# Three edits to when loads are issued in a hybrid attention and RWKV-7 block

## The chip, the cores and the metric

The kernel runs on one core of a Trainium2 chip. The metric is device time in microseconds (us) of one execution. PE is TensorE, PEld its weight load, DVE is VectorE, ACT is ScalarE, POOL is GpSimd, SP is SyncE, whose queue issues most DMA transfers. SPq in a row is SP's instruction queue.

## The reference

One decoder block over x (512 tokens, width 1024), all in float32:

```python
proj = rms_norm(x, norm_mix_g) @ w_in
o_nsa = nsa_attention(...)          # 8 heads: compressed, selected and window branch
o_rwkv = rwkv7_time_mix(...)        # 8 heads: recurrence over time, then
                                    # (layer norm of y + bonus) * gate
x = x + concatenate([o_nsa, o_rwkv]) @ w_out
x = x + memory_cross_attention(rms_norm(x, norm_x_g), rms_norm(mem, norm_mem_g), w_q_x, w_kv_x, w_o_x)
h = rms_norm(x, norm_ffn_g)
x = x + (silu(h @ w_gate) * (h @ w_up)) @ w_down
return rms_norm(x, norm_f_g)
```

The bonus is `sum(r * k * r_k) * v` for each head. x enters twice: at the start, and as the residual that is added to the output projection.

## The kernel before

Every large product is made of three: a float32 operand is split into a rounded high half and the remaining low half (`split`, lines L339 and L340: a cast on ACT, a subtraction on DVE), and high by high, high by low and low by high are summed.

The work is written as strands, Python generators that a planner (`Threads`) steps through. `start` loads x and norms it. `bulk` does all weight products, item by item, in the order of the text `ORDER`: r, K, q, v are parts of the input projection, m the compression, X and V the keys and values of the memory, `o00` to `o07` and `o10` to `o17` the output projection (first digit: the half of the tokens; second: the step over its 8 blocks of rows, which take the blocks 0 1 2 4 5 6 7 3), `x` the load of the residual, N the next norm, W a wait. Four strands `pair 0` to `pair 3` prepare the RWKV heads, `inverse` inverts their triangular matrices, `chain` runs the recurrence over 8 chunks and then, in a tail of four rounds, norms it, adds the bonus, multiplies by the gate and makes the output blocks 4 to 7. `attention` makes blocks 0 to 3. `mem` norms the memory.

The planner has a clock of its own, a priority for each strand, counts of free buffers by pool (Q, T, U and others) and a table of pauses (`ADJ`) by strand and number of the step. A strand that yields a dict of counts waits for that many free buffers; one that yields a number pauses. The order in which the planner steps the strands becomes the program order, which is the priority of the instructions. The language's scheduler then simulates the program and fixes the order of each engine's instructions and the buffer that each tile gets. An edge made by `after` orders only the issue: the scheduler places an instruction no earlier than the one named; on the chip nothing waits for it.

`pin` chains each strand's products in their own order; it stores the last product of any strand in `last[0]` and that of the strand in `mine`. `now` orders a load behind `last[0]`. It is used for weight loads (`wload`, L373), the bonus store (L650), the stores of the pairs (L669), the inverse's load (L713), the gate matrix (`gup`, L844) and the bonus loads (`bon`, L848).

The raw weights have two buffers (`tW`), their halves two each. `bulk` makes the halves of item n+1 and issues the load of item n+2 before the products of item n, so a weight load waits for the low half (L340) of the tile two items ahead of it. `xr_load` (L1314) loads the four tiles of x in one item between V03 and o00; they are added to the finished sums in `wout_item` (L1307). In the tail of `chain` each round takes three U buffers, loads the bonus first (L848), makes the variance, its rsqrt (L858, L859), the scaled row (L861, L862), adds the bonus on POOL (L863) and multiplies by the gate (L868). `inverse` stores its result at L729 and L730 and loads it back at L738 and L742.

Of the kernel before, what the change touches and what calls it, by code (L numbers as in the profile page):

```python
# [14 lines left out]
T = 512  # L15
# [43 lines left out]
INV_LAG = 9.0  # L59
DENS = 4500  # L60
PR = {'pair': 50}
ORDER = """L B P0 r00 r01 C1 r02 P1 r10 P2 r11 C0 r12 r21 m0 r20 m1 r22 P3 m2 r31 m3 r30 m4 r32 m5 K0 m6 q0 K1 m7 v0 v1 v2 q1 q3 q2 M X0 X1 X2 X3 X4 X5 X6 X7 V00 V01 V02 V03 x o00 o01 o02 o03 o04 o05 o06 o07 N o10 o11 o12 o13 o14 o15 o16 o17 W V10 V11 V12 V13"""


class Threads:
# [62 lines left out]
def _body(ctx, tc, I, out, dbg=None, upto=99, mark=lambda s: None):  # L128
    nc = tc.nc
# [13 lines left out]
    def mk(tag, bufs, pool=None):  # L143
        def f(shape=(128, 512), dt=F32, n=tag):
            return (pool or pp).tile(list(shape), dt, tag=tag, bufs=bufs, name=nm(n))
        return f
# [7 lines left out]
    tQ = mk("Q", NQ)  # L154
    tT = mk("T", NT)
    tU = mk("U", NU)
# [9 lines left out]
    th = Threads(mark, lambda n: tc.high_priority(n) if n else nullcontext(), Q=NQ - 7, T=NT, U=NU, K=KU, S=2, A=2)  # L166
# [4 lines left out]
    def after(ins, first):  # L171
        tc.add_manual_dep(ins.ins, first.ins.name,
                          mybir.DependencyInfo(mybir.DependencyClass.NoSync, mybir.DependencyReason.DATA), reason="order")
        return ins

    last, mine = [None], {}
# [8 lines left out]

    def now(ins):

        return after(ins, last[0]) if last[0] is not None else ins

    def free(ap):  # L190
        n = 1
# [4 lines left out]
    def mm(o, l, r, start, stop):  # L196
        m, n = free(l), free(r)
        if l.dtype == F32R:
            c = (0.055 if m <= 64 else 0.107) if n <= 128 else n * 0.000422
        elif m <= 32:  # L200
            c = 0.04
        elif m <= 64:
            c = max(0.08, n * 0.0009 + 0.02)
        else:
            c = max(0.214, n * 0.00168)
        th.cols.append((th.clock, n * l.shape[0] / 128 * (1 if l.dtype == F32R else F4)))
        return pin(PE.matmul(o, lhsT=l, rhs=r, start=start, stop=stop, skip_group_check=True), c)  # L207
# [157 lines left out]
    def qpair(n):  # L365
        t = tQ([128, 2, 512], F32R, n=n)
        return t[:, 0, :], t[:, 1, :]
# [203 lines left out]
    bdr = dp.tile([4, 128, 512], F32, name="bdr")  # L571
# [207 lines left out]
    def chain():  # L779
        yield "vt"  # L780

        def own(q):

            for c in (2 * q, 2 * q + 1):
                for j, e, o in HEADS:
                    r = slice(64 - o, 128 - o)
                    mm(pE[o:o + 64, c % 2, j, :], AM[j][e][r, c, 0:64], VT[c // 4][r, c % 4, j, :], True, True)
            z = tU([128, 2, 4, 64], n="zv")
            A.copy(z, pE)
            return z  # L790

        yield "vg"
        yield dict(A=1)
        pE = pA([128, 2, 4, 64], n="zy")
        zv = own(0)
        yield CH_LAG
        p = pC([128, 2, 4, 64], n="ch")
        S = None
        for c in range(8):

            uv = tU([128, 2, 4, 64], n="uv")
            G.tensor_copy(uv[64:128, 0], VT[c // 4][64:128, c % 4])
            G.tensor_copy(uv[0:64, 1], VT[c // 4][0:64, c % 4])
            if c > 0:
                for j, e, o in HEADS:
                    mm(p[o:o + 64, 0, j, :], AR[j][o:o + 64, c, 0:64], S[o:o + 64, j, :], True, True)
                Z = t1([128, 4, 64], n="Z")
                V.tensor_add(Z, p[:, 0], zv[:, c % 2])
            else:
                Z = zv[:, 0]  # L810
            if c % 2 == 1 and c < 7:
                zv = own(c // 2 + 1)
            if c > 0:
                yield CH_LAG
            for j, e, o in HEADS:
                mm(p[o:o + 64, 1, j, :], AM[j][e][o:o + 64, c, 0:64], Z[o:o + 64, j, :], True, True)
            V.tensor_copy(uv[0:64, 0], p[0:64, 1])
            A.copy(uv[64:128, 1], p[64:128, 1])
            if c > 0:
                for j, e, o in HEADS:  # L820
                    mm(pE[o:o + 64, c % 2, j, :], S[o:o + 64, j, :], AR[j][o:o + 64, c, 64:128], j == 0, False)
            yield CH_LAG

            Sn = None
            if c < 7:
                for j, e, o in HEADS:
                    mm(p[o:o + 64, 0, j, :], BKt[j][:, c, e, :], uv[:, e, j, :], True, True)
                Sn = t1([128, 4, 64], n="S")
                if c == 0:
                    V.tensor_copy(Sn, p[:, 0])  # L830
                else:
                    G.tensor_tensor(Sn, S, WC[:, :, c:c + 1].broadcast_to([128, 4, 64]), op=ALU.mult)
                    V.tensor_add(Sn, p[:, 0], Sn)
            for j, e, o in HEADS:
                mm(pE[o:o + 64, c % 2, j, :], uv[:, e, j, :], AM[j][e][:, c, 64:128], c == 0, True)
            A.copy(VT[c // 4][:, c % 4], pE[:, c % 2])
            S = Sn
            yield CH_LAG
        th.done("chain", 1.0)
        th.free(Q=16, U=4, A=1)  # L840

        yield dict(Q=1)
        gup = tQ([128, 512], n="gup")
        now(nc.sync.dma_start(gup, I["rwkv_g_up"][0]))  # L844
        for j in range(4):
            yield dict(U=3, T=2)
            bon, sq, rs = tU(n="bon"), tU(n="ysq"), tU(n="rs")
            now(nc.sync.dma_start(bon, bdr[j]))  # L848
            h2 = [slice(0, 256), slice(256, 512)]
            c4 = lambda x: x.rearrange("p (c t) -> p c t", c=4)  # L850
            for h in range(2):
                A.activation(c4(sq[:, h2[h]]), VT[h][:, :, j, :], AF.Square)
            bs = bsum(sq, "var", tT)
            yield next(bs) + 1.0
            yield dict(s=1)
            p = next(bs)
            th.free(T=2)
            A.activation(rs, p, AF.Ln, bias=kst[:, 1:2], scale=1.0 / 64)  # L858
            A.activation(rs, rs, AF.Exp, scale=-0.5)  # L859
            for h in range(2):  # L860
                V.tensor_mul(c4(rs[:, h2[h]]), c4(rs[:, h2[h]]), VT[h][:, :, j, :])  # L861
            V.tensor_scalar(rs, rs, col("rwkv_lnx_w", j), col("rwkv_lnx_b", j), op0=ALU.mult, op1=ALU.add)  # L862
            G.tensor_tensor(rs, rs, bon, op=ALU.add)  # L863
            yield 6.0
            yield dict(s=1)
            p = pS(n="g")
            mm(p, gup[:, j * 128:(j + 1) * 128], sgd, True, True)
            V.tensor_mul(rs, p, rs)  # L868
            yield dict(Q=1)
            oT[4 + j] = qpair("oT")  # L870
            split(*oT[4 + j], rs)
            th.free(U=3)
            th.done(f"o{4 + j}", 4.0)
        th.free(Q=3)
# [395 lines left out]
    xr, acc = [], {}  # L1270
# [40 lines left out]
                    th.free(Q=8, S=2)  # L1311
        return ld, run

    def xr_load(dep):  # L1314
        for i in range(4):
            xr.append(tQ([128, 1024], n="xr"))
            after(nc.sync.dma_start(xr[i], I["x"][0, i * 128:(i + 1) * 128, :]), dep)

    def norm_all(name, f, g, ev, done):
        name.append(f)  # L1320
# [26 lines left out]
    def xq_part(k):  # L1347
        return [(ALLP, 0, wcols("w_q_x", k * 128, 128))]
# [200 lines left out]
    def call(f, need=None):  # L1549

        def run(W):
            if need:
                yield need
            f()
        return None, run
# [9 lines left out]
    def build(n):  # L1565
        k, i = n[0], [int(c) for c in n[1:]]
        return {"L": lambda: duo(xn1, "xn", ([(ALLP, 0, wcols("w_in", RW0 + 1536, 128))], pA, lora_fin),
                                 ([(ALLP, 0, wcols("w_in", RW0 + 1664, 128))], pA, gd_fin)),
                "P": lambda: spawn_pair(*i), "r": lambda: rkv_item(*i), "B": lambda: call(lambda: th.add(1, "bias", bias(), th.clock)),
                "C": lambda: cv_item(*i), "m": lambda: cmp_item(*i), "K": lambda: k_item(*i),  # L1570
                "v": lambda: vg_item(*((0, 3), (3, 6), (6, 8))[i[0]]), "q": lambda: q_item(*i),
                "M": lambda: call(lambda: th.add(4, "mem", mem_load(last[0]), th.clock)),
                "X": lambda: kx_item(*i), "W": lambda: wait("chain"), "V": lambda: vx_item(*i),
                "x": lambda: call(lambda: xr_load(last[0]), dict(Q=4)),
                "o": lambda: wout_item(*i), "N": lambda: call(x_norm, dict(Q=9))}[k]()

    def x_norm():
# [4 lines left out]

    items = [build(n) for n in ORDER.split()]
    items += [duo(lambda: xn2[0], "xn2", (xq_part(0), pA, xq_fin(0), dict(Q=1)), (xq_part(1), pA, xq_fin(1), dict(Q=1)))] + \
# [55 lines left out]
```

## Time and profile before

| what | us |
|---|---|
| median of 3 runs | 959.26 |
| lowest and highest | 958.56 and 960.78 |
| the profiled execution | 957.83 |
| its span, from the first to the last instruction | 955.5 |

The profiled execution is one run; what lies around its span is 2.33 us. Durations below are from it, and the predicted time is set against the median of the runs.

### The profile page before, as it was taken

Reading aid. Unit: us, or ns where it says so; the run is one execution under the profiler, and the core shown is the slowest. Engines: PE = TensorE matmul, PEld = TensorE weight load, DVE = VectorE, ACT = ScalarE, POOL = GpSimd, SP = SyncE. Lnnn points to the kernel's source line nnn. Section 1 sums busy time; section 2 is a strip of 40 time slices with the busy share of each in tenths; the row PEclk is TensorE's granted clock in tenths of the full one; section 3 lists DMA queues with packets and bytes.
Section 4 is the critical chain, followed back from the end, with each engine's and each line's share of the span. In section 5 each row is a group of like instructions: output and inputs, shape, how many; then the busy total and the mean of one; then the engine's idle time right before and its main releaser. Section 6 shows DMA issues by size and latency. Waiting matters only on the chain.

```text
span 955.5 us, 14534 instructions
## 1 busy us (share of the span) xinstructions
PE 910.5 (95%) x5797; PEld 741.0 (78%) x5797; DVE 508.4 (53%) x991; ACT 401.2 (42%) x738; POOL 81.7 (9%) x128
## 2 busy tenths in 40 slices
PE   6999999999999988799899999999999999999997
PEld 4778777777778766666788888888888888888885
DVE  5366676788566776356655555444343343422235
ACT  4455444347567886234444433332333323212121
POOL 5121110000240010001200002000000000000002
PEclk9999999999999999999999999999999999999999
DMA  7222445636203111754431141333333333242332
GB/s 229 60 63 70 128 108 144 174 89 133 91 2 101 35 56 45 220 176 153 134 88 46 65 139 39 110 89 91 109 88 110 89 90 109 88 131 89 95 105 88
DMA packets 125405, 97.19 MB, mean 102 GB/s; under 512 B 23531, under 2 KB 109873, under 8 KB 125339
## 3 DMA queue, kind: packets, MB, share of 16 engines
q1 hardware_dynamic: 122714, 91.80, 33.2%
q10 hardware_dynamic: 2624, 4.48, 1.7%
q8 instruction: 45, 0.74, 0.3%
q14 instruction: 22, 0.17, 0.1%
HBM read 90.22 MB, written 4.48 MB: 99 GB/s over the span
## 4 chain that ended last, share of the span: by engine, by line
PE 76%; DVE 7%; ACT 6%; DMA 5%; issue 3%; POOL 2%; SPq 0%; POOLq 0%; ACTq 0%; DVEq 0%
PE pj L207 41%; PE acc L207 14%; DMA w<-in_w_out_dram 3%; PE pv L207 2%; DVE wl L340 2%; ACT wh L339 2%; PE sc L207 2%; PE pt L211 2%; PE ps L207 1%; PE vg L207 1%; PE ch L207 1%; DMA w<-in_w_kv_x_dram 1%; PE kx L207 1%; PE xs L207 1%; PE xo L207 1%
## 5 line engine op out<-in xcount | busy, mean ns | idle before, releaser
L207 PE MATMUL pj<-xn,wh 128*128 128x512 f32 (+1 forms) x1280 | 294.3, 378 | 0.5 <-DVE xn L340 0.5
L340 DVE TENSOR_TENSOR wl<-w,wh 128x1024 fp32r<-128x1024 f32 (+1 forms) x130 | 158.4, 1219 | 203.7 <-ACT wh L339 118.9
L207 PEld LDWEIGHTS pj<-xn,wh 128*128 128x128 f32 x1280 | 227.9, 190 | 46.0 <-issue 2.9
L339 ACT CAST wh<-w 128x1024 fp32r<-128x1024 f32 (+1 forms) x131 | 136.9, 1045 | 284.7 <-PE pj L207 144.6
L207 PE MATMUL pj<-xn,wl 128*128 128x512 f32 (+1 forms) x640 | 155.3, 379 | 0.0
L207 PEld LDWEIGHTS pj<-xn,wl 128*128 128x128 f32 x640 | 114.2, 189 | 22.0 <-issue 1.6
L207 PE MATMUL acc<-wh,hid 128*128 128x512 f32 x288 | 68.2, 389 | 0.0
L207 PEld LDWEIGHTS acc<-wh,hid 128*128 128x128 f32 x288 | 54.1, 188 | 11.2
L1475 DVE SCALAR_TENSOR_TENSOR th<-th,pj 128x512 f32<-128x512 f32 x22 | 15.1, 688 | 75.7 <-PE pj L207 75.7
L207 PE MATMUL acc<-wh,oT 128*128 128x512 f32 x128 | 34.6, 410 | 7.1 <-ACT wh L339 4.5
L1105 ACT ACTIVATE S<-S,mx 128x128 f32<-128x128 f32 (+3 forms) x64 | 35.3, 553 | 4.3 <-DVE mx L1103 4.2
L207 PEld LDWEIGHTS acc<-wh,oT 128*128 128x128 f32 x128 | 23.5, 192 | 15.8 <-ACT wh L339 7.9
L207 PE MATMUL acc<-wl,hid 128*128 128x512 f32 x144 | 35.6, 389 | 0.0
L1536 POOL TENSOR_TENSOR xr<-xr,gain 128x512 f32<-128x512 f32 x4 | 5.2, 1290 | 345.4 <-DVE ss L1533 345.4
L1103 DVE CUSTOM_DVE_ANT_0 S<-ps,Bt 128x128 f32<-128x128 f32 (+3 forms) x64 | 29.7, 484 | 8.5 <-PE ps L207 8.3
L207 PE MATMUL ps<-K,q 128*128 128x512 f32 (+2 forms) x96 | 30.1, 395 | 3.4 <-DVE mx L1103 2.3
L207 PEld LDWEIGHTS acc<-wl,hid 128*128 128x128 f32 x144 | 27.0, 188 | 5.6
L207 PE MATMUL pv<-S,Vt 128*64 128x128 f32 x320 | 30.6, 284 | 0.3 <-ACT S L1146 0.2
L211 PE MATMUL pt<-ident,S 128*128 128x128 f32 x160 | 25.8, 280 | 4.2 <-ACT S L1146 4.2
L339 ACT CAST hid<-th 128x512 fp32r<-128x512 f32 x22 | 13.7, 621 | 31.7 <-DVE th L1475 31.7
L280 POOL TENSOR_TENSOR ss<-ss,kst 128x1 f32<-128x1 f32 x14 | 7.7, 552 | 208.3 <-DVE ss L279 208.3
L211 PEld LDWEIGHTS pt<-ident,S 128*128 128x128 f32 x160 | 18.1, 140 | 9.4 <-ACT S L1146 5.3
(298 smaller groups left out, 1303.2 us busy)
## 6 DMA issues: line engine op xcount, KB each, us to landing
w<-in_w_gate_dram SPq DMA_DIRECT2D x22, 512.0 KB, 3.9
w<-in_w_up_dram SPq DMA_DIRECT2D x22, 512.0 KB
w<-in_w_down_dram SPq DMA_DIRECT2D x22, 512.0 KB, 3.4
w<-in_w_in_dram SPq DMA_DIRECT2D x18, 512.0 KB, 5.4
w<-in_w_kv_x_dram SPq DMA_DIRECT2D x16, 512.0 KB, 4.6
w<-in_w_out_dram SPq DMA_DIRECT2D x16, 256.0 KB, 3.9
w<-in_w_out_dram SPq DMA_DIRECT2D x8, 512.0 KB, 5.0
w<-in_w_q_x_dram SPq DMA_DIRECT2D x8, 512.0 KB, 3.9
```

Source lines behind the costliest of these rows:

```text
L207: return pin(PE.matmul(o, lhsT=l, rhs=r, start=start, stop=stop, skip_group_check=True), c)
L211: return pin(PE.transpose(o, i, idn), 0.109 if i.shape[0] > 64 else 0.056)
L280: G.tensor_tensor(ss[:, 1:2], ss[:, 0:1], mhalf, op=ALU.pow)
L339: seq(A, A.copy(H, src))
L340: i = (eng or V).tensor_sub(L, src, v32(H))
L1103: V.tensor_tensor_reduce(out=s, in0=p[:, br - b0], in1=Bt[:, a, n - 1::-1], scale=-1.0, scalar=3e38, op0=ALU.add, op1=ALU.min, accum_out=m ...
L1105: A.activation(s, s, AF.Exp, bias=mx[:, a, br + 1:br + 2], scale=-1.0, accum_out=sm[:, a, br + 1:br + 2])
L1475: V.scalar_tensor_tensor(t, t, 0.5, p, op0=ALU.mult, op1=ALU.mult)
L1536: G.tensor_tensor(x, x, gf[0][:, cs], op=ALU.mult)
```

## The change

A load that went through `now` is ordered behind the last product of its own strand, and behind the last of any strand only if its own has none yet. The bonus is loaded after the row is scaled, and its U buffer is asked for there. The load of the residual becomes four items, one ahead of each pair of the first half's parts of the output projection, each asking for one Q buffer instead of four at once.

```diff
-... V02 V03 x o00 o01 o02 o03 o04 o05 o06 o07 N ...
+... V02 V03 x0 o00 o01 x1 o02 o03 x2 o04 o05 x3 o06 o07 N ...
...
     def now(ins):
 
-        return after(ins, last[0]) if last[0] is not None else ins
+        own = mine.get(th.cur, last[0])
+        return after(ins, own) if own is not None else ins
...
         for j in range(4):
-            yield dict(U=3, T=2)
-            bon, sq, rs = tU(n="bon"), tU(n="ysq"), tU(n="rs")
-            now(nc.sync.dma_start(bon, bdr[j]))
+            yield dict(U=2, T=2)
+            sq, rs = tU(n="ysq"), tU(n="rs")
...
             V.tensor_scalar(rs, rs, col("rwkv_lnx_w", j), col("rwkv_lnx_b", j), op0=ALU.mult, op1=ALU.add)
+            yield dict(U=1)
+            bon = tU(n="bon")
+            now(nc.sync.dma_start(bon, bdr[j]))
             G.tensor_tensor(rs, rs, bon, op=ALU.add)
...
-    def xr_load(dep):
-        for i in range(4):
-            xr.append(tQ([128, 1024], n="xr"))
-            after(nc.sync.dma_start(xr[i], I["x"][0, i * 128:(i + 1) * 128, :]), dep)
+    def xr_load(i, dep):
+        xr.append(tQ([128, 1024], n="xr"))
+        after(nc.sync.dma_start(xr[i], I["x"][0, i * 128:(i + 1) * 128, :]), dep)
...
-                "x": lambda: call(lambda: xr_load(last[0]), dict(Q=4)),
+                "x": lambda: call(lambda: xr_load(*i, last[0]), dict(Q=1)),
```

## Rows read from the trace of the kernel before

**Rows 1.** The page's first part: busy us (share of the span) xinstructions.
```profile
PE 910.5 (95%) x5797; PEld 741.0 (78%) x5797; DVE 508.4 (53%) x991; ACT 401.2 (42%) x738; POOL 81.7 (9%) x128
```
**Rows 2.** Windows: stretch, length, busy us by engine, granted clock, DMA share, GB/s.
```profile
240.00:300.00 60.00, 59.01 (x1086) 47.70 (x1085) 38.02 (x128) 37.05 (x105) 16.21 (x31) 1.00 0.19 62
...
395.00:410.00 15.00, 12.13 (x44) 9.36 (x45) 4.70 (x5) 3.10 (x3) 0.00 (x0) 0.89 0.73 240
...
600.00:825.00 225.00, 225.00 (x995) 186.27 (x993) 89.19 (x105) 69.03 (x84) 0.00 (x0) 1.00 0.34 98
```
**Rows 3.** Waits of PE, 20 to 380: us in total, times, longest.
```profile
PE ps L207 <- DVE mx L1103: 2.3, 1, 2.3
...
PE kx L207 <- ACT wh L339: 0.6, 1, 0.6
```
**Rows 4.** Waits of PE, 380 to 470.
```profile
PE acc L207 <- ACT wh L339: 4.5, 6, 2.3
PE acc L207 <- DVE vx L340: 2.7, 1, 2.7
PE acc L207 <- DVE wl L340: 1.6, 2, 1.1
```
**Rows 5.** Timeline of PE, 386 to 426: start, us, work [idle before <-releaser].
```profile
402.01 1.07 PE L207 MATMUL acc<-wl,oT 128*128 128x512 f32 x4
405.38 2.11 PE L207 MATMUL acc<-wh,oT 128*128 128x512 f32 x8 [2.30 <-ACT wh L339]
...
408.23 1.98 PE L207 MATMUL acc<-wh,oT 128*128 128x512 f32 x8
...
411.47 2.11 PE L207 MATMUL acc<-wh,oT 128*128 128x512 f32 x8 [0.36 <-ACT wh L339]
...
417.72 2.12 PE L207 MATMUL acc<-wh,oT 128*128 128x512 f32 x8 [0.51 <-ACT wh L339]
```
**Rows 6.** Timeline of ACT, 402 to 424.
```profile
404.28 2.05 ACT L339 CAST wh<-w 128x1024 fp32r<-128x1024 f32 x2 [7.02 <-DMA w<-in_w_out_dram]
410.37 1.05 ACT L339 CAST wh<-w 128x1024 fp32r<-128x1024 f32 x1 [4.04 <-DMA w<-in_w_out_dram]
...
416.62 1.05 ACT L339 CAST wh<-w 128x1024 fp32r<-128x1024 f32 x1 [3.30 <-DMA w<-in_w_out_dram]
```
**Rows 7.** Timeline of SP's queue, in short windows from 386 to 414.
```profile
391.58 3.00 SPq L1317 DMA_DIRECT2D xr<-in_x_dram  x4
394.94 3.94 SPq L373 DMA_DIRECT2D w<-in_w_out_dram  x3
...
406.61 0.33 SPq L373 DMA_DIRECT2D w<-in_w_out_dram  x1
...
412.70 0.33 SPq L373 DMA_DIRECT2D w<-in_w_out_dram  x1
```
**Rows 8.** Timeline of SP's queue, 200 to 300.
```profile
215.71 0.34 SPq L729 DMA_DIRECT2D ydr<-yb  x1
...
232.78 2.00 SPq L373 DMA_DIRECT2D w<-in_w_kv_x_dram  x2
...
286.27 0.33 SPq L844 DMA_DIRECT2D gup<-in_rwkv_g_up_dram  x1
...
287.13 0.43 SPq L373 DMA_DIRECT2D w<-in_w_kv_x_dram  x1
```
**Rows 9.** Timeline of DVE, 225 to 227 and 371 to 380.
```profile
225.53 1.22 DVE L340 TENSOR_TENSOR wl<-w,wh 128x1024 fp32r<-128x1024 f32 x1
...
372.16 0.68 DVE L340 TENSOR_TENSOR oT<-rs,oT 128x512 fp32r<-128x512 f32 x1
```
**Rows 10.** Timeline of POOL, 300 to 375.
```profile
367.74 2.05 POOL L863 TENSOR_TENSOR rs<-rs,bon 128x512 f32<-128x512 f32 x1 [16.74 <-DVE rs L862]
```
**Rows 11.** Instructions of one tile, var: duration ns min/median/max, first and last start.
```profile
L207 PE MATMUL var<-bl,bones_r x4: 387/396/401, 305.5 to 360.0; 128*128 128x512 f32 x4
```
**Rows 12.** DMA issues: count, KB each, median us to landing.
```profile
gup<-in_rwkv_g_up_dram SPq DMA_DIRECT2D x1, 256.0 KB, 2.7
```

More of the change, by code (lines that the diff above doesn't have):

```diff
@@ L61 @@
 PR = {'pair': 50}
-ORDER = """L B P0 r00 r01 C1 r02 P1 r10 P2 r11 C0 r12 r21 m0 r20 m1 r22 P3 m2 r31 m3 r30 m4 r32 m5 K0 m6 q0 K1 m7 v0 v1 v2 q1 q3 q2 M X0 X1 X2 X3 X4 X5 X6 X7 V00 V01 V02 V03 x o00 o01 o02 o03 o04 o05 o06 o07 N o10 o11 o12 o13 o14 o15 o16 o17 W V10 V11 V12 V13"""
+ORDER = """L B P0 r00 r01 C1 r02 P1 r10 P2 r11 C0 r12 r21 m0 r20 m1 r22 P3 m2 r31 m3 r30 m4 r32 m5 K0 m6 q0 K1 m7 v0 v1 v2 q1 q3 q2 M X0 X1 X2 X3 X4 X5 X6 X7 V00 V01 V02 V03 x0 o00 o01 x1 o02 o03 x2 o04 o05 x3 o06 o07 N o10 o11 o12 o13 o14 o15 o16 o17 W V10 V11 V12 V13"""
 class Threads:
```

## The prediction, written before the changed kernel ran

> **What bounds the kernel now.** I read the page first, then the stretches, then PE's waits, then the timelines of the engines around each edited load. The page says that PE is busy for 95% of the span [rows 1], so a change can only pay where PE stands still. The stretches show where that is. From 600 to 825 PE never stops, from 240 to 300 it stops for one microsecond in 60, and from 395 to 410 it works for 12.13 of 15 us at a granted clock of 0.89, with the DMA engines at 0.73 of their time [rows 2]. That last stretch is the output projection, the place where the change puts the loads of x.
>
> PE's waits tell the two halves apart. Between 20 and 380 us the longest wait is 2.3 us on VectorE, and the only wait that names a weight tile is 0.6 us [rows 3]: loads are not what PE lacks there. Between 380 and 470 PE waits 4.5 us for ScalarE's cast of a weight tile and 1.6 us for VectorE's low half of one [rows 4], 6.1 us together. Both casts stand behind a load, because the raw weights have two buffers and the load of tile n+2 starts when the low half of tile n is made.
>
> The timelines show the worst of these waits. Each part of the projection is 12 products; part o02 runs from 405.38 to 408.23, 2.85 us [rows 5]. PE ended o01 at 403.08 and stood 2.30 us until the cast of o02, and later parts wait 0.36 and 0.51 us [rows 5]. The cast of o02 starts at 404.28, after 7.02 us in which ScalarE waited for the DMA [rows 6]. SyncE issued the four loads of x at 391.58 and the load of o02 at 394.94, right behind them [rows 7].
>
> **The change part by part.**
>
> *Loads of x, one before each pair of parts.* The same four loads of 512 KB are issued. From the issue of o02's load to its cast pass 404.28 - 394.94 = 9.34 us. With no x ahead the same takes 410.37 - 406.61 = 3.76 us and 416.62 - 412.70 = 3.92 us [rows 6, 7]. So four x loads cost o02 some 5.5 us, 1.4 us each. After the change only x0 stands ahead: cast of o02 near 394.94 + 3.9 + 1.4 = 400.2, high half ready at 401.3, before PE ends o01 at 403.08. The 2.30 us wait goes.
>
> What x1, x2 and x3 then cost is bounded from both sides. x1 has no wait of its own, so SyncE issues it directly behind the load of o03; the load of o04 can only be issued when o02's low half is made (cast 1.05 us [rows 6], low half 1.22 us [rows 9]), some 3 us later. If x1 has landed by then, it costs nothing, and so for x2 and x3: the upper end is that all waits of PE on the casts go, 4.5 us [rows 4]. If instead each x still adds its 1.4 us to the weight load behind it, one buffer's round takes 3.9 + 1.05 + 1.22 + 1.4 = 7.6 us instead of the 6.1 to 6.25 us between the casts at 404.28, 410.37 and 416.62 [rows 6]. Starting at 400.2, three such rounds end at 423.0; before, one more round of 6.2 us after 416.62 ends at 422.8. The gain has then been paid back: 0. I take 2.3 us, the one wait that is caused by the pile of x loads, and leave the small repeating ones in place, since they come every part, x or not.
>
> On those small waits the Trainium skill, Perfetto Trace Analysis, section Optimization Strategy, says that a gap which repeats through a stretch can mean that buffers are too few. By it the 0.36 and 0.51 us waits belong to the two weight buffers, which the change leaves alone, and the sum stays at 2.3 us rather than 4.5. The trace agrees so far as that both recur where no x load is near.
>
> *Loads ordered behind the strand's own last product.* The order is one of issue only; no semaphore is added. On the chip such a load waits for its buffer, so the edit can only change its place in SyncE's queue and, through the scheduler, the order on the other engines. Weight loads may move up: the one at 232.78 stands behind the inverse's transfers from 215.71 on, the one at 287.13 behind the load of the gate matrix at 286.27 [rows 8]. I cost this at nothing, because the 59.01 of 60 us of PE work in 240 to 300 [rows 2] are there without these loads. Its ends: a gain, if weight work moved up fills PE's later gaps; a loss, if a weight load that waits for its buffer now stands ahead of a transfer that the recurrence needs. Both are rivals below.
>
> *Bonus loaded late.* Four loads move from the head of a round to just before the add that reads them; each waits for one free scratch buffer. It is ordered behind the round's variance product, not behind the add. In the last round that product starts at 360.0 [rows 11] and the add at 367.74 [rows 10], 7.7 us apart; a load of the same size landed in 2.7 us [rows 12]. Hidden with 5 us to spare. A late bonus would hold POOL's add, then DVE's multiply (L868), and behind that on DVE the low halves of weight tiles. If the cover were gone, 2.7 us would be added to each of four rounds, 11 us to the recurrence's tail. Its last output is split at 372.16 [rows 9] and is first read by part o06 at 417.72 [rows 5], so even that has 45 us of room. The raw scratch need of a round falls from three to two and one; the planner's numbered pauses shift by one per round. Its strand is late by fractions of a microsecond at most, in front of the same 45 us: nothing.
>
> **Sum.** The profiled execution took 957.83 us, 2.33 more than its span of 955.5. 957.83 - 2.3 = 955.5 us. The median of the runs is 1.43 us above the profiled one, so 959.26 - 2.3 = 957.0 us.
>
> **The rivals.**
>
> *A, the forecast:* the pile is gone, the rest hidden. 957.0, from 954.8 (4.5 us) to 959.3 (0).
>
> *B, the same bytes in the same queue:* each x still holds up the weight load behind it, as in the lower bound; 959.3. For it speaks that the DMA engines are at 0.73 in 395 to 410 [rows 2]; against it that x1 is issued some 3 us ahead of the next weight load. The Trainium skill, DMA: Bandwidth & Descriptors, section Queues, rings and completion order, says that each DMA engine takes a ring's descriptors in order. By that rule a load behind x pays for x wherever x stands in the queue, and the time would be 959.3. The trace agrees for the pile (9.34 against 3.8 us); for a single x with a pause behind it no row here shows it.
>
> *C, more than the forecast:* weight loads that no longer wait for other strands let projection work start under the attention's cover, and all of PE's waits on weights in 380 to 470 go: 4.5 + 1.6 = 6.1 us [rows 4], 953.2. For it speaks that weight loads were held for long behind other transfers [rows 8]; against it that no PE wait before 380 asks for weights [rows 3].
>
> *D, slower:* SyncE is one queue. The inverse's store goes out at 215.71 [rows 8], and the weight tile whose buffer is needed next gets its low half only at 225.53 to 226.75 [rows 9]. If the load into that buffer comes ahead of the store, everything behind the inverse starts up to 226.75 - 215.71 = 11.0 us later, and PE, which takes its products in a fixed order, stands in front of the recurrence. It decides as soon as that one weight load is ahead of the store in the queue. Half of it hidden: 957.0 + 5.5 = 962.5; none hidden: 968. Against it: the scheduler places a load when it believes its buffer to be free.
>
> **How the numbers follow.** A has 0.42, B 0.18, C 0.18, D 0.22. About 0.2%, 1.9 us, is what can be told from no change here: faster is below 957.3, slower above 961.2. A lies across the first bound, 0.24 faster, 0.15 same, 0.03 slower; B gives 0.03, 0.10, 0.05, since a reshuffled order has a spread of its own; C is faster, 0.18; D gives 0.03 same and 0.19 slower. Sums: faster 0.45, same 0.28, slower 0.27. The range takes in C at 953.2 and D half hidden at 962.5 and leaves out D in full: 952 to 964. A's own range is 954.8 to 959.3.
>
> **What the profile after would show.** Right: the x loads stand one by one between weight loads on SyncE's timeline, the cast of o02 follows its load within 5.5 us, and PE's wait between o01 and o02 is gone while the waits of later parts stay below 1 us. B: waits of 1 us or more before o04, o06 and o10. C: X tiles and projection parts on PE well before 380. D: a weight load with a long wait on SyncE ahead of the inverse's or the bonus's transfers, and PE idle before the recurrence's products. I am wrong if the difference comes from 20 to 380 us, through an order of instructions that these rows can't show.

## The result, and the profile after

The changed kernel takes 967.17 us (median of 4 runs, 965.88 to 970.61) against 959.66 us for the kernel before, timed beside it. The ratio is 1.0072, with a 95% interval from 1.0048 to 1.0097: slower, and above the whole predicted range of 952 to 964. The profiled execution took 970.61 us, 12.8 us more than the profiled one of before, so it shows somewhat more loss than the 7.5 us between the medians.

I read the profile after in the order in which I had read the one before. First the page: busy us (share of the span) xinstructions, and the packets, MB and share of the instruction queue.

```profile
PE 920.0 (95%) x5797; PEld 749.9 (77%) x5797; DVE 508.5 (52%) x991; ACT 400.7 (41%) x738; POOL 77.2 (8%) x128
...
q8 instruction: 45, 0.74, 0.3%
```

PE has the same 5797 products as in [rows 1], yet is busy 9.5 us longer. The work is the same, so some of it ran slower. Then the stretches: busy us by engine, granted clock, DMA share, GB/s.

```profile
68.00:84.00 16.00, 14.38 (x103) 12.28 (x104) 10.25 (x14) 4.76 (x8) 2.81 (x4) 0.79 0.29 71
...
240.00:250.00 10.00, 8.99 (x233) 7.25 (x233) 3.34 (x10) 3.31 (x9) 1.58 (x4) 0.99 0.66 205
250.00:268.00 18.00, 16.07 (x160) 11.61 (x159) 6.91 (x22) 6.18 (x19) 1.92 (x5) 0.53 0.01 2
...
600.00:825.00 225.00, 225.00 (x1045) 188.39 (x1044) 89.26 (x109) 70.44 (x86) 1.84 (x2) 1.00 0.32 94
```

From 600 to 825 nothing has changed against [rows 2]. The loss is in 240 to 268, the stretch that the prediction had called full. Before, 240 to 300 had a clock of 1.00 throughout [rows 2]; now it is 0.53 from 250 to 268. At the two levels of the clock, 2.4 GHz (1.00) and 1.2 GHz (0.50), a mean of 0.99 over 10 us and 0.53 over 18 us are 0.2 + 16.9 = 17.1 us at half clock. The stretch from 68 to 84 reads 0.79 too: 6.7 us at half clock. The same reading of 0.79 is in the profiles of now_hold, which loses no time (below), and of before_early, and it is not in that of before (1.00), so I put it down to the execution and not to the change.

What PE did before the clock fell is on its timeline (start, us, work, [idle before <-releaser]). These are the small products of `inverse`.

```profile
244.82 1.10 PE L208 MATMUL lt<-X,AM 32*32 32x32 f32 x57
...
247.41 0.69 PE L208 MATMUL y<-AM,LT 32*32 32x32 f32 x32
248.04 0.65 PE L208 MATMUL pv<-S,Vt 128*64 128x128 f32 x6
248.62 0.43 PE L208 MATMUL y<-AM,LT 32*32 32x32 f32 x14
251.93 0.64 PE L208 MATMUL y<-AM,LT 32*32 32x32 f32 x16 [2.88 <-issue]
252.50 0.69 PE L208 MATMUL ch<-zv,AM 64*64 64x64 f32 x8
```

In the middle of one run of 30 like products PE stands still for 2.88 us, and "issue" says that the profile shows nothing that it waits for: no semaphore, and so no other engine, holds it. That row carries the whole case. The kernel before makes the same 30 products in one piece:

```profile
244.81 0.85 PE L207 MATMUL y<-AM,LT 32*32 32x32 f32 x30
```

What else is going on at that moment is on SP's queue, after and then before.

```profile
206.84 0.37 SPq L374 DMA_DIRECT2D w<-in_w_kv_x_dram  x1
...
235.95 2.32 SPq L374 DMA_DIRECT2D w<-in_w_kv_x_dram  x2
243.41 0.35 SPq L1202 DMA_DIRECT2D mem<-in_norm_mem_g_dram  x1
243.80 0.90 SPq L1205 DMA_DIRECT2D mem<-in_mem_dram  x2
```

```profile
238.54 0.35 SPq L1199 DMA_DIRECT2D mem<-in_norm_mem_g_dram  x1
250.87 0.37 SPq L373 DMA_DIRECT2D w<-in_w_kv_x_dram  x1
251.29 1.05 SPq L1202 DMA_DIRECT2D mem<-in_mem_dram  x2
```

Before, a weight load stood on SP's queue between the memory norm's gain and the two loads of the memory, waited 11.9 us for its buffer until 250.87, and held the memory back behind it. With each load ordered behind its own strand, the weight loads have moved up by one: the first of them now goes out at 206.84, three of them and not two stand ahead of the gain, and none stands between it and the memory. So the memory, some 1.5 MB with its gain, goes out in one piece at 243.4 to 244.7, its two large loads one microsecond before the burst of small products.

The DMA view of the kernel after (queue, kind: packets, MB, share of 16 engines), first from 244 to 249, then from 249 to 251; and the kernel before from 242 to 244:

```profile
q1 hardware_dynamic: 374, 1.40, 90.3%
...
q1 hardware_dynamic: 58, 0.18, 22.7%
q8 instruction: 1, 0.02, 3.2%
```

```profile
q8 instruction: 1, 0.02, 3.6%
```

The queue q8 of kind "instruction" moves 45 packets, 0.74 MB in all, 16,384 bytes each. Spread over PE's 5797 products and 5797 weight loads that is 63.6 bytes for each, and the packets keep step with PE: between the starts of the 10th, 11th and 12th in the kernel after, PE starts 261 and 244 instructions. So I read them as PE's own instructions, brought in block by block by the same DMA engines that carry the data. In the packet records of the trace the 13th of them starts 1.59 us after the burst of small products begins in the kernel before (242.82 against 241.23). In the kernel after it starts 4.72 us behind it (249.54 against 244.82), 3.1 us late, when the bulk of the memory is through, and PE goes on 1.4 us after it has landed (250.57, then 251.93).

One count in the traces speaks for a block's end and against anything in the products themselves. When PE stops it has started 3521 instructions: 1735 products, 1736 weight loads and 50 others, nearly all for semaphores. It is the same 3521 in the other two kernels below that stop: now_alone with the same three numbers, and before_early, where PE's order is another, with 1736, 1737 and 48.

So the reading is: memory on the DMA engines, block of instructions late, PE out of instructions for 2.88 us, half clock for 17.1 us around and behind that. If work that PE bounds loses half of the time at half clock, that is 8.6 us; with the stop 11.4 (an estimate: the trace's clock falls at 249.8, so some of the stop itself lies in the half clock). Part o00 starts 12.3 us later than before (407.86 against 395.57): 11.4 and the 3.4 us of the stretch at 72 make 14.8. Of the 2.5 us between, 1.8 came back from 200 to 220, where before has a clock of 0.91 and after 1.00; the rest I have not followed.

The x loads did what was forecast. The waits of PE from 390 to 450 and the first of those from 20 to 390 (us in total, times, longest), then SP's queue:

```profile
PE acc L208 <- ACT wh L340: 5.4, 4, 3.1
...
PE acc L208 <- DVE vx L341: 1.2, 1, 1.2
...
PE y L208 <- issue: 2.9, 1, 2.9
```

```profile
400.00 3.82 SPq L374 DMA_DIRECT2D w<-in_w_out_dram  x4
403.88 1.50 SPq L1319 DMA_DIRECT2D xr<-in_x_dram  x1
...
411.06 0.43 SPq L1319 DMA_DIRECT2D xr<-in_x_dram  x1
...
417.03 0.42 SPq L1319 DMA_DIRECT2D xr<-in_x_dram  x1
```

The wait of 2.30 us between o01 and o02 [rows 5] is gone: from o00's start at 407.86 PE has no wait over 0.6 us until o10. The load of o02, issued at 407.23, is cast at 411.91, 4.7 us behind it, within the 5.5 us forecast. The wait at o10 is the 3.1 us in the first of these rows; the last experiments take it up.

### The profile page after: what moved, and what is told of

Its sections match the earlier page's. It is cut to its first block, busy times and chain, and to the rows that moved or that the text cites. A ratio compares the mean times of both kernels' runs of the same rounds, so it can differ in the third digit from the quotient of the medians.

```text
span 968.6 us, 14529 instructions
## 1 busy us (share of the span) xinstructions
PE 920.0 (95%) x5797; PEld 749.9 (77%) x5797; DVE 508.5 (52%) x991; ACT 400.7 (41%) x738; POOL 77.2 (8%) x128
## 4 chain that ended last, share of the span: by engine, by line
PE 48%; DMA 4%; DVE 3%; ACT 2%; issue 1%; POOL 1%; SPq 0%; POOLq 0%; ACTq 0%; DVEq 0%
PE pj L208 29%; PE acc L208 15%; DMA w<-in_w_out_dram 2%; DVE wl L341 1%; PE xs L208 1%; PE xo L208 1%; ACT wh L340 1%; DMA w<-in_w_down_dram 1%; PE vx L208 1%; DMA gain<-in_norm_x_g_dram 1%; PE tr L212 1%; DMA w<-in_w_up_dram 1%; DMA w<-in_w_kv_x_dram 0%; PE xpt L212 0%; POOL xs L295 0%
## 5 line engine op out<-in xcount | busy, mean ns | idle before, releaser
L208 PEld LDWEIGHTS pv<-S,Vt 128*64 128x64 f32 x320 | 20.2, 139 | 6.9 <-issue 2.3
```

## The experiments

Times are medians of 6 to 12 runs of each kernel beside 24 to 35 of the kernel before on the same chip, ratios with 95% intervals. The kernels were run in three sets, each on a chip of its own: the first four of the table, the next four, the last three. The medians of before are 960.45, 960.34 and 959.90, so kernels of different sets are compared by their ratios, which are not always the ratio of the two medians.

| kernel | what it is | us (lowest to highest) | ratio to before |
|---|---|---|---|
| x_alone | before + loads of x one by one | 958.31 (955.15–960.71) | 0.9981 [0.9961, 1.0001] |
| now_alone | before + own-strand order | 968.49 (964.38–972.07) | 1.0091 [1.0062, 1.0120] |
| bon_alone | before + late bonus | 960.22 (955.28–963.78) | 0.9997 [0.9975, 1.0020] |
| x_bon | the change without own-strand order | 958.18 (953.78–962.79) | 0.9985 [0.9961, 1.0008] |
| now_hold | now_alone, memory loads held back | 960.16 (956.97–963.37) | 1.0000 [0.9976, 1.0023] |
| now_small | now_alone, memory loads cut to 1/64 | 962.73 (958.58–965.96) | 1.0026 [1.0002, 1.0049] |
| before_early | before, memory loads earlier | 965.40 (962.54–972.15) | 1.0062 [1.0037, 1.0087] |
| after_hold | the change, memory loads held back | 959.68 (956.16–962.77) | 1.0004 [0.9980, 1.0028] |
| x_early | x_alone, x1 to x3 further forward | 954.98 (953.48–957.83) | 0.9936 [0.9914, 0.9958] |
| x_gain | x_early + norm gain loaded early | 954.06 (953.04–958.81) | 0.9947 [0.9924, 0.9969] |
| xb_gain | x_gain + late bonus | 956.80 (952.63–959.77) | 0.9958 [0.9936, 0.9979] |

### Which of the three edits

Each edit was put alone into the kernel before, and the two that looked harmless together.

x_alone:

```diff
-... V02 V03 x o00 o01 o02 o03 o04 o05 o06 o07 N ...
+... V02 V03 x0 o00 o01 x1 o02 o03 x2 o04 o05 x3 o06 o07 N ...
...
-                "x": lambda: call(lambda: xr_load(last[0]), dict(Q=4)),
+                "x": lambda: call(lambda: xr_load(*i, last[0]), dict(Q=1)),
```

> The kernel before with one edit: the four loads of x stand one by one between pairs of parts of the output projection. Theory 1 (the time is lost where the memory loads, moved up, meet the burst of 32x32 products at 242 to 250 us; x is innocent): the first half of the projection, from the start of o00 to the start of o10, takes some 2 us less than the 29.2 us of before; 955 to 958 us, faster by 0.1 to 0.4%. Theory 2 (x and the load of the norm's gain collide at o10, 3.14 us of PE idle and a low clock behind it, and this costs the time): no gain or slower, 960 to 964. In both there is no half clock between 245 and 270.

now_alone:

```diff
-        return after(ins, last[0]) if last[0] is not None else ins
+        own = mine.get(th.cur, last[0])
+        return after(ins, own) if own is not None else ins
```

> The kernel before with one edit: loads ordered behind their own strand's last product. Theory 1: this edit carries the loss. The memory loads are issued some 7 us earlier, directly ahead of the 32x32 products, PE stands 2 to 3 us inside that burst with no semaphore to wait for, and the granted clock is half for some 17 us behind it: 966 to 971 us, slower by 0.7 to 1.2%. Theory 2: within 0.3% of before. Theory 3 (the bonus, loaded late, holds the recurrence's tail): within 0.3% of before.

bon_alone:

```diff
-            yield dict(U=3, T=2)
-            bon, sq, rs = tU(n="bon"), tU(n="ysq"), tU(n="rs")
-            now(nc.sync.dma_start(bon, bdr[j]))
+            yield dict(U=2, T=2)
+            sq, rs = tU(n="ysq"), tU(n="rs")
...
+            yield dict(U=1)
+            bon = tU(n="bon")
+            now(nc.sync.dma_start(bon, bdr[j]))
             G.tensor_tensor(rs, rs, bon, op=ALU.add)
```

> The kernel before with one edit: the bonus is loaded after the scaled row is made and its scratch buffer is asked for there. Theory 1: within 0.3% of before, 957 to 962, and no stop of PE in the burst of 32x32 products. Theory 3: slower, with waits of POOL's add for the bonus load and of the engines behind it, 963 to 970.

x_bon is the changed kernel with `now` as it was:

```diff
-        own = mine.get(th.cur, last[0])
-        return after(ins, own) if own is not None else ins
+        return after(ins, last[0]) if last[0] is not None else ins
```

> The change without its first edit: x split and the bonus late, loads still ordered behind the last product of any strand. Theory 1: about the sum of the two, 955 to 959 us, no stop of PE between 240 and 252 and no half clock there. Theories 2 and 3: slower than before, 962 to 970.

Measured: the own-strand order alone gives 1.0091, more than the whole change. The other two together are at 0.9985, not told apart from no change. So the loss comes with the edit that the prediction costed at nothing. PE in now_alone, its stop, and its granted clock from 240 to 250 and from 250 to 268:

```profile
245.41 0.43 PE L208 MATMUL y<-AM,LT 32*32 32x32 f32 x14
248.77 0.64 PE L208 MATMUL y<-AM,LT 32*32 32x32 f32 x16 [2.92 <-issue]
```

```profile
240.00:250.00 10.00, 7.02 (x217) 5.74 (x215) 2.36 (x5) 2.33 (x6) 1.58 (x4) 0.82 0.52 159
250.00:268.00 18.00, 17.67 (x227) 13.18 (x225) 11.86 (x34) 9.76 (x29) 5.11 (x9) 0.81 0.01 4
```

It is the same stop, after the same 14 products. The memory went out at 240.6, one microsecond before the burst at 241.62. At half clock are 3.6 + 6.8 = 10.4 us; half of them and the stop are 8.1 us, and the medians are 8.0 apart (968.49 against 960.45). That the two agree so closely is in part luck: the profile is of one execution, at 964.38 us the shortest of the six. The expectation had some 17 us at half clock, as in the kernel after.

### Is it the memory's transfer, or the order of everything else?

The own-strand order moves many instructions, not only one load: of PE's 5797 products 732 stand at another place than in before. The theory is that the transfers of the memory, next to the burst, keep PE's instructions from arriving. The rival is that the new order of the products, casts or stores costs the time, and that the stop is only where it shows. Four kernels tell them apart: two that keep the new order and take the transfer out of the way, one that keeps the old order and puts the transfer in the way, and the whole change with the transfer out of the way.

now_hold holds the two loads of the memory until the last of the small products is issued and copied out; a copy of one element into their tile makes the wait real. (The pauses of `mem` in the planner's table are renumbered, and one of them, of 2.9, is dropped.)

```diff
             yield 0
+        th.done("y12")
         th.add(0, "chain", chain(), th.clock + 1.0)
...
+        yield "y12"
         for i in range(2):
             mt.append(tmp[:, i])
+            A.copy(tmp[0:1, i, 0:1], AM[3][0][0:1, 0, 32:33])
             after(nc.sync.dma_start(mt[i], I["mem"][0, i * 128:(i + 1) * 128, :]), dep)
```

> Loads ordered behind their own strand, as in now_alone, and the two loads of the memory (512 KB each) held until the inverse's last products are done, by a one-element copy on ScalarE into their tile; every other instruction stands in the order of now_alone on PE, DVE and POOL. Theory 1 (the memory loads keep the DMA engines busy when PE needs its next block of instructions): PE's stop of 2.9 us in the burst is gone, no half clock behind it, 957 to 962 us, level with before. Theory 4 (the new order of products itself costs the time): stays at 966 to 971.

now_small keeps the place of the loads and takes away their size:

```diff
+            G.memset(mt[i][:, 16:1024], 0.5)
-            after(nc.sync.dma_start(mt[i], I["mem"][0, i * 128:(i + 1) * 128, :]), dep)
+            after(nc.sync.dma_start(mt[i][:, 0:16], I["mem"][0, i * 128:(i + 1) * 128, 0:16]), dep)
```

> now_alone with the memory loads cut to 16 of 1024 columns; the rest of the memory is a constant, so cross attention reads other data. The order of instructions is that of now_alone on PE, DVE and ACT. Theory 1: no stop in the burst, 956 to 962 us. Theory 4: 966 to 971.

before_early is the kernel before, in which the loads of the memory are issued when the strand `mem` is started, not at its first step. On SP's queue the two loads and the weight load change places; the other engines keep their order.

```diff
-    def mem_load(dep):
+    def mem_first(dep):
         tmp = tX([128, 3, 1024], n="mem")
...
+        return gm
+
+    def mem_load(gm):
...
-                "M": lambda: call(lambda: th.add(4, "mem", mem_load(last[0]), th.clock)),
+                "M": lambda: call(lambda: th.add(4, "mem", mem_load(mem_first(last[0])), th.clock)),
```

> The kernel before, with nothing moved but the two memory loads and one weight load in SyncE's queue: the memory loads are traced when the memory strand is started and so stand ahead of the weight load that held them up. Every other engine has the order of before. Theory 1: PE stops 2 to 3 us within the 32x32 products at 241 to 246, the clock is half for 10 to 17 us behind it, 965 to 971 us. Theory 4: within 0.3% of before, 957 to 963.

after_hold is the changed kernel with the three lines of now_hold and the same pauses.

> The whole change, with the memory loads held as in now_hold. Theory 1: the loss is gone and the 2 us of the split x loads remain: 955 to 960 us, faster than before by 0 to 0.4%. Theory 4: 965 to 970, as the change.

Measured: with the memory held back the loss is gone, in now_hold (1.0000) and in the whole change (1.0004). With the memory brought forward the kernel before loses 0.62%, with nothing else moved. The traces show the orders that the comparison needs: PE's products stand in the order of now_alone in now_hold and now_small, and in before_early all engines but SP keep the order of before, where two entries of SP's queue differ; in after_hold 12 of PE's 5797 products stand elsewhere than in after. So the rival falls as the cause of the loss: the transfer without the new order costs 5 us, and the new order without the transfer nothing that the ratios show (a share of about 1 us comes up below).

Three expectations were not met in full. before_early stops for 1.37 us where 2 to 3 were expected, with 6.9 us at half clock where 10 to 17 were. now_small's 962.73 is just above its 956 to 962. after_hold is level with before, so the 2 us of the x loads that were expected to remain do not show in its time. SP's queue and PE in before_early:

```profile
240.35 0.35 SPq L1199 DMA_DIRECT2D mem<-in_norm_mem_g_dram  x1
240.75 0.90 SPq L1202 DMA_DIRECT2D mem<-in_mem_dram  x2
255.93 0.38 SPq L373 DMA_DIRECT2D w<-in_w_kv_x_dram  x1
```

```profile
243.04 1.10 PE L207 MATMUL lt<-X,AM 32*32 32x32 f32 x57
...
246.62 0.47 PE L207 MATMUL y<-AM,LT 32*32 32x32 f32 x17
248.46 0.38 PE L207 MATMUL y<-AM,LT 32*32 32x32 f32 x13 [1.37 <-issue]
```

The same in now_hold:

```profile
242.67 0.35 SPq L1201 DMA_DIRECT2D mem<-in_norm_mem_g_dram  x1
252.59 0.82 SPq L1206 DMA_DIRECT2D mem<-in_mem_dram  x2
```

```profile
244.09 1.10 PE L208 MATMUL lt<-X,AM 32*32 32x32 f32 x57
...
247.88 0.69 PE L208 MATMUL y<-AM,LT 32*32 32x32 f32 x30
```

The 30 products that are 14 + 16 in the kernel after and 17 + 13 in before_early run in one piece. The granted clock of these two and of now_small, from 240 to 250 and from 250 to 268:

```profile
240.00:250.00 10.00, 8.57 (x254) 6.86 (x253) 3.32 (x9) 2.40 (x6) 1.58 (x4) 0.98 0.70 213
250.00:268.00 18.00, 17.75 (x274) 13.41 (x272) 10.71 (x30) 10.40 (x28) 3.80 (x7) 0.82 0.11 31
```

```profile
240.00:250.00 10.00, 9.94 (x264) 7.93 (x263) 3.43 (x10) 3.99 (x10) 1.58 (x4) 1.00 0.27 84
250.00:268.00 18.00, 17.31 (x285) 13.61 (x286) 14.11 (x44) 11.67 (x39) 5.11 (x9) 1.00 0.17 62
```

```profile
240.00:250.00 10.00, 9.94 (x238) 7.70 (x237) 3.01 (x6) 4.39 (x9) 3.40 (x6) 1.00 0.18 57
250.00:268.00 18.00, 17.31 (x341) 14.06 (x342) 15.16 (x47) 11.21 (x38) 6.66 (x13) 1.00 0.01 4
```

In before_early 0.4 + 6.5 = 6.9 us are at half clock; half of them and the stop are 4.8 us, and the medians are 5.1 apart (965.40 against 960.34). Neither stop nor fall of the clock is in the other two, nor in after_hold (1.00 in both stretches). That now_small has no stop though its loads are issued at the same place (gain at 240.19, memory at 240.59, burst at 241.6) says that the bytes matter and not the place in the queue. Its 1.0026, with a lower end at 1.0002, is left over; the profile shows no cause for it, and its memsets and its norm of a constant are other work too.

The start of the 13th instruction packet behind the start of the burst, from the packet records, completes the picture:

| kernel | burst begins | packet starts | behind it | PE's stop |
|---|---|---|---|---|
| before | 241.23 | 242.82 | 1.59 | none |
| x_bon | 241.12 | 242.71 | 1.59 | none |
| now_hold | 244.09 | 245.75 | 1.66 | none |
| before_early | 243.04 | 246.07 | 3.03 | 1.37 |
| after | 244.82 | 249.54 | 4.72 | 2.88 |
| now_alone | 241.62 | 246.47 | 4.85 | 2.92 |

Against 1.6 us the packet is 1.4, 3.1 and 3.2 us late in the three last, and PE stands for 1.37, 2.88 and 2.92. That ties the stop to the late packet.

### What the loads of x are worth

x_alone's 0.9981, 1.8 us, is near the 2.3 us forecast, but its interval reaches 1. In its profile the waits of PE from 390 to 450 for a cast are two, where before has six from 380 to 470 [rows 4]:

```profile
PE acc L207 <- ACT wh L339: 3.5, 2, 2.3
```

None of them is at o02 or up to o07 any more: PE waits 1.20 us at o10 and 2.32 us at o12, where the load of x3 and that of the next norm's gain have just gone out. (The expectation of x_early below puts the 2.3 us before o10; it is before o12.) x_early puts x1 to x3 further forward, away from there:

```diff
-... V02 V03 x0 o00 o01 x1 o02 o03 x2 o04 o05 x3 o06 o07 N ...
+... V02 V03 x0 o00 x1 o01 o02 x2 o03 x3 o04 o05 o06 o07 N ...
```

> x_alone with the loads of x moved further forward, so that the last stands ahead of o04 instead of o06 and meets neither the load of o10 nor that of the norm's gain. If the 2.3 us wait of PE before o10 in x_alone comes from the last x load standing ahead of o10's load, it falls below 1.5 us and the time is 955 to 958, 0.2 to 0.4% under before. If it comes from the gain's load alone, the wait stays at 2 us or more and the time is that of x_alone, 957 to 960.

x_gain also loads the norm's gain ahead, on SP before o05 (item `G`, which asks for one of the norm's nine Q buffers), not on ACT at the norm:

```diff
-... o03 x3 o04 o05 o06 o07 N ...
+... o03 x3 o04 G o05 o06 o07 N ...
...
-    def x_norm():
-        g, i = gain("norm_x_g")
+    def gx_load():
+        g, i = gain("norm_x_g", nc.sync)
         after(i, last[0])
+        gxl.append(g)
+
+    def x_norm():
+        g = gxl[0]
```

> x_early with the gain of the cross-attention norm loaded on SyncE's queue ahead of o05's turn instead of from ScalarE at the end of o07. If the gain's load is what o10 waits for, the wait before o10 is under 1 us and the time 953 to 957, 0.3 to 0.6% under before; if not, as x_early.

xb_gain is x_gain with the late bonus, as in bon_alone.

> x_gain with the bonus loaded late as well. Since the bonus edit alone measured no difference: within 0.2% of x_gain.

Measured: x_early 0.9936, x_gain 0.9947, xb_gain 0.9958. All three are faster than before and than the change; among themselves their intervals overlap. PE in x_early at o11; then in x_gain at o11 and in o12:

```profile
426.13 2.14 PE L207 MATMUL acc<-wh,oT 128*128 128x512 f32 x8 [2.83 <-ACT wh L339]
```

```profile
424.72 2.11 PE L207 MATMUL acc<-wh,oT 128*128 128x512 f32 x8 [0.66 <-ACT wh L339]
...
431.95 1.21 PE L207 MATMUL acc<-wl,oT 128*128 128x512 f32 x4 [1.08 <-DVE wl L340]
```

The early gain takes all but 0.66 us of the 2.83 us wait away, with PE's products in the same order, so that wait came with the gain's load. In the changed kernel the profile puts the 3.1 us at o10 down to the same load: the cast for o10 stood 5.11 us behind it on ACT.

```profile
427.59 0.34 ACTq L226 DMA_DIRECT2D gain<-in_norm_x_g_dram  x1
433.72 1.04 ACT L340 CAST wh<-w 128x1024 fp32r<-128x1024 f32 x1 [5.11 <-DMA gain<-in_norm_x_g_dram]
```

There the load of x3 stands directly ahead of that of o10 on SP's queue as well (424.05 and 426.25). x_early, where x3 is further forward, has no wait at o10, so a share of x3 in the wait at o10 is not ruled out.

By the ratios x_gain is no faster than x_early, so the wait was not the price that it looked like. x_early's median is 3.3 us below x_alone's. From o00 to o10 the two profiles take 24.52 and 25.22 us, against 29.17 before: 0.7 us of difference. The rest is in large part the draw of the clock. Up to 230 us the two kernels issue the same instructions in the same order, yet the granted clock there is 0.98 in x_early's profile and 0.95 in x_alone's, some 7 us of time in these two executions.

The times can be compared at equal clock. A straight line through the runs of before, time against mean granted clock, falls by 0.76 to 0.77 us for each 0.001 in all three sets, with a scatter of about 1 us. This comparison is an estimate, and it is fair only to kernels whose edit doesn't itself change the clock much. Set against the line of their own set, the runs of x_alone are 2.0 us lower in the mean, x_bon 2.0, bon_alone 0.4, x_early 3.1, x_gain 3.0 and xb_gain 2.7, each uncertain by 0.6 to 1 us. So the x loads one by one are worth about 2.0 us, clear of zero and close to the forecast, and x_early about one more, which is hardly told apart from none. now_hold is 1.0 us above the line of its set, now_small 2.0 and after_hold 0.1: the new order without the transfer costs perhaps 1 us, which hides part of what the x loads gain in after_hold.

## Why the prediction was wrong, point by point

**The step that failed** is the second edit, "Loads ordered behind the strand's own last product", and its sentence "I cost this at nothing, because the 59.01 of 60 us of PE work in 240 to 300 are there without these loads". The term measured 8.0 us (now_alone). The steps up to it were right: the edit adds no semaphore, it changes places on SP's queue and the order on the other engines, and weight loads moved up. The conclusion was not. That PE is 98% busy in a stretch says that no wait is left there to gain, not that nothing can be lost there: with no idle time to take it up, PE's stop of 2.9 us cost its length and then the half clock behind it. I asked only whether PE lacked weights there, and not what else a transfer that moves can meet on the DMA engines. It was the memory, which I had not listed among the loads that move, because `now` does not order it: it moved because the weight load ahead of it in the queue did. With the memory held back the same edit measured 1.0000, so what the term left out is the memory's transfer ahead of the burst, PE's late block of instructions and the clock that fell.

**Rival D** gave a time that was measured, 962.5 to 968, by a mechanism that was not seen; that its range holds the time is luck. Its condition did come about, a weight load ahead of the inverse's store on the queue (206.84 against 219.97), but that load's buffer was free in time: the store waited 12.7 us for DVE's result, 15.0 before. PE had no wait for the inverse's result. SP did wait longer in one place, 54.6 us for the gate matrix's buffer where before had 34.1, but PE waits for nothing behind it. The waits of SP's queue in the kernel after:

```profile
SPq L845 <- DVE pcT L1137: 54.6, 1, 54.6
...
SPq L865 <- POOL pc L1084: 32.6, 3, 17.1
```

**The loads of x**: forecast 2.3 us. The wait at o02 went as worked out, and o00 to o10 became 3.95 us shorter in x_alone's profile (29.17 to 25.22) and 2.2 in that of the change (26.95). In the time x_alone's gain is 0.19% or 1.8 us, with an interval that holds both 0 and 3.7, and at equal clock about 2.0. Rival B, that every x is paid wherever it stands, is not borne out by the profile: in the kernel after, o01 to o07 have no wait over 0.6 us. Of its signs only a wait at o10 appeared, where the gain's load comes in too. The small waits that I left standing and put down to the two weight buffers are gone in x_alone, with the same two buffers: there o01 to o07 have no wait at all. So that attribution does not hold there; what took their place is 1.20 us at o10 and 2.32 at o12. (x_bon's profile has 1.26 us at o07 as well.) That 2.3 us is near the measured gain is therefore in part luck.

**The bonus**: forecast nothing, measured 0.9997 [0.9975, 1.0020]. The second row above shows its waits: SP stands up to 17.1 us for a free buffer before a bonus load. That is not new, before had such waits of up to 17.6 us. They hold nothing up: in the profile after POOL's adds wait for DVE's row or for PE and never for a bonus load. So the cover held, as worked out.

**Rival C** does not hold for the change. Its 953.2 was approached only by another order, x_gain's 954.06.

**The last sentence of the prediction**, that it would be wrong if the difference came from 20 to 380 us through an order that these rows can't show, is what happened. The trace of before could have shown it in part: the timeline of SP's queue had the memory behind a weight load that waited, and PE's the burst of 190 small products right there.

## What to carry to other kernels

Where an edit moves a load, list everything that stands behind it on its queue: those transfers move too, and their new neighbours are what to look at. In these traces PE's instructions come over the same DMA engines as the data. In a dense burst of tiny products PE needs its next block of instructions soon: here 190 products and as many weight loads in 4.4 us. A megabyte of bulk in front of that burst starved it with no semaphore to be seen. Look for "issue" ahead of a long idle time of PE inside a run of like products, and try to hold the bulk until behind the burst; in now_hold that took the loss away. And compare runs at equal clock where a difference is half a per cent.

## What the runs showed of the hardware that was not expected

- A block of PE's instructions is 16 KB (45 packets, 0.74 MB), and one was 3.1 us late while the data queue held 90.3% of the 16 DMA engines. The Trainium skill, Runtime: NRT & Kernel Launch, section Instruction fetch mechanics, says that instructions come in blocks of 16 KiB and that crossing a block's end is mostly hidden. The size agrees; hidden it is in before, x_bon and now_hold (no stop in the table), and not in the three kernels with the whole memory ahead of the burst (1.37, 2.88 and 2.92 us). Whether the block's request was made late or waited its turn behind data on the DMA engines no run here tells.
- The stop is the smaller part of its price. With stops of 1.37, 2.92 and 2.88 us went 6.9, 10.4 and 17.1 us at half clock, worth 3.4, 5.2 and 8.6 us by the estimate above. Why the lengths differ is left open.
- The time of one kernel follows its granted clock. Among the 29 runs beside x_alone the kernel before took 955.0 us at a mean clock of 0.993 and 964.99 at 0.982. That is 1% between executions of one kernel, so one run alone can't tell a difference of half a per cent.
